# Loading attention's values per pair of heads, more buffers for the squares of the out-projection, and the refill's low parts on one engine

## The chip, the cores and the metric

The kernel runs on one core of a Trainium2 chip. The metric is the device time of one execution in microseconds (us), here the median of three runs. All arithmetic on TensorE (PE) that has to be accurate is done in three passes: a float32 operand is cut into a high part (a rounded copy) and a low part (the difference), and high times high, high times low and low times high are summed. The high part is a cast on ScalarE (ACT), the low part a subtraction on VectorE (DVE) or on GpSimd (POOL). SyncE (SP), ACT and POOL each issue DMA transfers into a queue of their own.

## What is computed

One decoder layer for 2048 tokens of width 1024, with 8 attention heads of 64:

```python
hn = _rmsnorm(h, ln_mix[i])
z = hn @ w_in[i]                                  # q, k, v and the pooling channels u
att = _dilated_attention(q, k, v, slopes)         # windows (128,1), (512,4), (2048,16)
pool = _multiscale_pool(u, pool_w[i], pool_scale[i])
h = h + jnp.concatenate([att, pool], axis=-1) @ w_out[i]
hn = _rmsnorm(h, ln_ffn[i])
up = _causal_dwconv(hn @ w_up[i], conv_w[i], conv_b[i])
gate, val = jnp.split(up, 2, axis=-1)
h = h + (jax.nn.silu(gate) * val) @ w_down[i]
g = jax.nn.sigmoid(_rmsnorm(h, ln_ple[i]) @ w_ple_gate[i])
h = h + g * (p[i] @ w_ple[i])
```

Each head's three dilated branches are summed by weights that come out of their row maxima and denominators.

## The kernel before, in words

The time line of the profiled execution has these stages: projection (0 to 401 us), attention (401 to 737), out-projection (737 to 945), up (945 to 1809), down (1809 to 2300), and gate, per-layer embedding and final norm (to the end).

**Attention** runs 8 heads of NQ = 16 steps each, in four pairs of 32 steps. A step computes the scores of one block (`far_scores`, `near_scores`), their maxima and exponentials, transposes them and multiplies by the values. The near branch reads tiles `v1`, the far ones `v3`, four of each per head. All operands come from DRAM through SP's queue: at the start `load_qk(0) + load_v(0)`, then the list `queue`, to which step 1 of each head appends the eight transfers of `load_qk(h + 1)` (six of 0.5 MB with rows of 8 KB, and the bias tiles `fb` and `nb`) and step 8 the eight of `load_v(h + 1)` (256 KB each, 512 bytes to a row); one is put in SP's queue per step. SP is in order: a transfer whose buffer is not yet free holds all that stand behind it. The score operands have one buffer for even and one for odd heads, so those of head h + 1 are free when head h - 1 ends; `v1` has 7 buffers and `v3` 6.

At the end of a pair, `mix_stats` stores the pair's statistics (`std`, `stf`) and loads them back in another layout (`sn`, `sf`); step 9 of the next pair computes from these (`mix_lift`, DVE tile `lo`), step 10 the weights, stored as `wd` (`mix_weights`). Then, for each of four chunks c, `mix_fetch` loads two tiles `wb` (the weights broadcast over 64 partitions), `mix_products` multiplies them with the sums s1 and s3 into m1 and m3 and adds these, and `mix_store` splits and stores the result. All of the mix's DMAs are issued by POOL, and its products run on POOL too: POOL is in order, so `std` and `stf` of the next pair stand behind the last chunk's products and stores.

**Out-projection.** Four token chunks c, each in two groups of four output tiles. `end(grp)` adds the residual (`xc`), stores h1 and calls `add_square`: ACT squares the tile into `sq`, DVE adds it to `acc`. After each chunk `rms_scale` sums `acc` over the partitions on PE (`st`).

**Up** is 44 turns, in each of which PE multiplies seven products; their operands a11, s2, a12, s1, s3, s4, a22 (normalised states and sums of them) stand in SBUF as high and low parts. The class `Refill` brings operands for the first half (12 of the 24 in a12, s3, a22 are still to come at its first turn) and, at turn NF - 1 to NF + 1, all 56 of the second half: a load by SP, the cast on ACT, the subtraction on POOL for each third (first refill) or each second (second refill), else on DVE. POOL also computes the weight sums of each turn (`sums_t`, `sum_t4`). In the step after the last turn (`over`) the last activations (`yg`) are finished while the first units of down are loaded and split (`unit0`, `unit1`, `unit2`).

Of the kernel before, what the change touches and what calls it, by code (L numbers as in the profile page):

```python
# [49 lines left out]
def fp(ap):  # L50
    return ap.bitcast(F32)
# [433 lines left out]
def phase_attention(tc, g, mx, near_b, far_b):  # L485
# [5 lines left out]
    with ExitStack() as ctx:  # L491
# [27 lines left out]

        def load_v(h):  # L520
            t = heads[h]
            near_v = g.vn.rearrange("n r j h a d -> (r j) n h (a d)")
            far_v = g.vf.rearrange("r (b m) j h a d -> r (m j) b h (a d)", m=4)
            t.v1, t.v3 = [], []
            loads = []
            for q in range(4):
                v1 = sb.tile([P, 4, P], F32R, tag="v1", bufs=7, name=f"v1_{h}_{q}")
                v3 = sb.tile([P, 4, P], F32R, tag="v3", bufs=6, name=f"v3_{h}_{q}")
                loads.append((v1, near_v[:, 4 * q : 4 * q + 4, h, :]))
                loads.append((v3, far_v[q, :, :, h, :]))  # L530
                t.v1.append(v1)
                t.v3.append(v3)
            return loads

# [84 lines left out]
        def near_pv(gi, kbs, first):  # L619
            gr, t, q0 = groups[gi], heads[gi // 4], 4 * (gi % 4)  # L620
            for kb in kbs:
                if q0 + kb < 0:
                    continue
                m0, m1 = max(0, kb), min(3, kb + 1)
                b0, b1 = 4 * m0 + kb + 1, 4 * m1 + kb + 1
                kt = q0 + kb
                for pt in (gr.h, gr.l):
                    nc.tensor.matmul(
                        gr.o[:, m0 * P : (m1 + 1) * P],
                        t.v1[kt // 4][:, kt % 4, :],  # L630
                        pt[:, b0 : b1 + 1 : 4, :],
                        start=first,
                        stop=False,
                        skip_group_check=True,
                    )
                    first = False

        def far_pv(gi, kbs, first):
            gr, t = groups[gi], heads[gi // 4]
            for kb in kbs:  # L640
                for pt in (gr.h, gr.l):
                    nc.tensor.matmul(
                        gr.o[:, kb * P :],
                        t.v3[gi % 4][:, kb, :],
                        pt[:, 6 * kb + 2 : 18 + kb : 5, :],
                        start=first,
                        stop=False,
                        skip_group_check=True,
                    )
                    first = False  # L650
# [67 lines left out]
        with tc.manual_schedule(engines=set(EN.values())):  # L718
            for dst, src in load_qk(0) + load_v(0):
                rdma(nc, dst, src)  # L720
            queue = []
            stages = {
# [3 lines left out]
            for s in range(NS + 10):  # L726
                if s < NS:
                    h, n = divmod(s, NQ)
                    if n == 1 and h + 1 < H:
                        queue += load_qk(h + 1)  # L730
                    if n == 8 and h + 1 < H:
                        queue += load_v(h + 1)
                    if queue:
                        rdma(nc, *queue.pop(0))
                if s == NS + 2:
                    last_far(nc, g, mx, ps_t, pairs[NPAIR - 1])
                    pieces = pairs[NPAIR - 1].pieces = last_weights(nc, mx, pairs[NPAIR - 1])
# [171 lines left out]
def phase_rest(tc, g, mxs, mx, last_pair, xT, pT, w_out, w_up, w_down, w_gate, w_ple, outT):  # L909
# [3 lines left out]
    with ExitStack() as ctx:  # L913
# [255 lines left out]
        for c in range(NCH):  # L1169
# [16 lines left out]
            def begin(grp):  # L1186
# [5 lines left out]
                for j in range(4):  # L1192
                    x = cb.tile([P, CH], F32, tag="xh1", bufs=10, name=f"xc{c}")
                    nc.sync.dma_start(x, xT[4 * grp + j, :, cs])
                    xs.append(x)

            def end(grp):
                for j in range(4):
                    jj = 4 * grp + j
                    nc.vector.tensor_tensor(xs[jj], pss[grp][j], xs[jj], op=ALU.add)  # L1200
                    nc.scalar.dma_start(g.h1[jj][:, cs], xs[jj])
                    add_square(nc, cb, acc, xs[jj], jj == 0)
                    hs.append(xs[jj])
# [113 lines left out]
        class Refill:  # L1317
            def __init__(self, half, names, depth, low):
                self.todo = [(p, k) for p in names for k in range(HK)]
                self.half, self.depth, self.low, self.got, self.n = half, depth, low, [], 0  # L1320

# [10 lines left out]
            def take(self, n=1):  # L1332
                for _ in range(n):
# [10 lines left out]
                    nc.scalar.copy(hi, t)  # L1344
                    (nc.gpsimd if m % self.low == self.low - 1 else nc.vector).tensor_tensor(lo, t, fp(hi), op=ALU.subtract)
                    if m:
# [24 lines left out]
        with tc.manual_schedule(engines=set(EN.values())):  # L1371
            raw_load(1)
            refill = Refill(0, ("a12", "s3", "a22"), 6, 3)
            for _ in range(6):
# [5 lines left out]
            for i in range(len(turns) + 1):  # L1380
# [7 lines left out]
                if i == NF - 1:  # L1388
                    assert not prep
                    refill = Refill(1, ("a11", "s2", "a12", "s1", "s3", "s4", "a22"), 10, 2)  # L1390
                    for _ in range(10):
                        refill.fetch()
# [35 lines left out]
                if prev:  # L1428
                    conv_b(prev.yv, prev.uv, NF + prev.f, prev.half)
                after(1)  # L1430
                if last:
# [55 lines left out]
                after(6)  # L1487
                if over:
                    unit2()
                prev = None if over else cur  # L1490
# [369 lines left out]
```

## Time and profile before

| | us |
|---|---|
| median of three runs | 2545.92 |
| the three runs | 2545.68, 2554.62, 2545.92 |
| profiled execution, its own time | 2557.69 |
| its span | 2555.8 |
| mean granted clock of PE | 0.971 |
| PE busy | 2428.2 (95%) |
| DVE busy | 1589.2 (62%) |
| ACT busy | 1106.9 (43%) |
| POOL busy | 556.7 (22%) |

The profiled execution is 11.8 us longer than the median of the runs and 3.1 us longer than the slowest of them. PE is busy nearly all the time, so what an edit can bring lies in PE's idle stretches and in stretches of a lower granted clock.

### The profile page before, as it was taken

The numbers are of one execution on the slowest core, as the hardware profiler recorded it, in microseconds if no ns is written. First come the engines' busy times: TensorE is split into PE (matmuls) and PEld (weight loads), VectorE is DVE, ScalarE is ACT, GpSimd is POOL, SyncE is SP. The second block draws the span as 40 slices with busy tenths as digits, with TensorE's granted clock in tenths as the row PEclk, the third lists the DMA queues.
The fourth block names the chain that finished last, engine by engine and source line by source line (L and its number), as shares of the span: only waits on it lengthen the run. The fifth ranks groups of instructions, "written<-read, shape, count | busy, mean of one in ns | idle before, by whom it ended". The sixth has DMA issues, their size and how long they took to land.

```text
span 2555.8 us, 31938 instructions
## 1 busy us (share of the span) xinstructions
PE 2428.2 (95%) x11515; PEld 2034.4 (80%) x11515; DVE 1589.2 (62%) x2396; ACT 1106.9 (43%) x1923; POOL 556.7 (22%) x454
## 2 busy tenths in 40 slices
PE   8999999888779998999999999999999999999998
PEld 7888887777667877888887888888788888887788
DVE  6645527867673466888889767666535373444654
ACT  5423327877641134444446444444323243333332
POOL 3312221144420023333343000000122222212010
PEclk9899999999889999999999999999999999999999
DMA  7534358697556664455556433433546464544332
GB/s 241 165 120 177 144 175 257 161 216 161 150 180 206 221 227 155 160 173 186 185 181 198 132 120 120 132 120 111 186 141 217 148 224 151 197 146 143 120 103 87
DMA packets 222831, 424.12 MB, mean 166 GB/s; under 512 B 39904, under 2 KB 82528, under 8 KB 219600
## 3 DMA queue, kind: packets, MB, share of 16 engines
q1 hardware_dynamic: 187616, 368.94, 45.7%
q0 software_dynamic: 18912, 25.75, 3.2%
q10 hardware_dynamic: 16144, 27.38, 2.9%
q8 instruction: 91, 1.49, 0.2%
q14 instruction: 68, 0.56, 0.1%
HBM read 290.01 MB, written 131.89 MB: 165 GB/s over the span
## 4 chain that ended last, share of the span: by engine, by line
PE 74%; DMA 8%; issue 7%; DVE 4%; ACT 2%; POOL 2%; SPq 0%; POOLq 0%; DVEq 0%; ACTq 0%
PE ua L1288 18%; PE uc L1288 9%; PE dn L89 6%; PE dn L90 6%; PE dn L88 6%; PE ub L1288 4%; DMA wb<-wd 4%; PE z L90 4%; PE z L88 4%; PE z L89 4%; PE o L88 2%; PE o L90 2%; PE o L89 2%; PE gp L90 2%; PE gp L88 2%
## 5 line engine op out<-in xcount | busy, mean ns | idle before, releaser
L88 PE MATMUL dn<-ah,hd 128*128 128x512 f32 x704 | 274.8, 390 | 2.7 <-ACT ah L83 2.7
L89 PE MATMUL dn<-al,hd 128*128 128x512 f32 x704 | 274.9, 390 | 1.9 <-DVE al L84 1.9
L90 PE MATMUL dn<-ah,ld 128*128 128x512 f32 x704 | 274.5, 390 | 0.0
L84 POOL TENSOR_TENSOR ld<-rd,hd 128x1024 fp32r<-128x1024 f32 x42 | 101.3, 2413 | 756.2 <-ACT hd L83 745.8
L83 ACT CAST hd<-rd 128x1024 fp32r<-128x1024 f32 x88 | 92.5, 1052 | 264.6 <-PE dn L89 226.2
L84 DVE TENSOR_TENSOR al<-ra,ah 128x512 fp32r<-128x512 f32 x88 | 120.3, 1371 | 134.0 <-ACT ah L83 134.0
L88 PE MATMUL z<-hnh,wh 128*128 128x512 f32 (+1 forms) x480 | 171.2, 357 | 9.7 <-ACT hnh L251 5.8
L89 PE MATMUL z<-hnl,wh 128*128 128x512 f32 (+1 forms) x480 | 170.9, 356 | 2.6 <-DVE hnl L252 2.5
L90 PE MATMUL z<-hnh,wl 128*128 128x512 f32 (+1 forms) x480 | 170.8, 356 | 2.3 <-POOL wl L84 1.7
L88 PEld LDWEIGHTS dn<-ah,hd 128*128 128x128 f32 x704 | 132.6, 188 | 30.8 <-ACT ah L83 3.1
L89 PEld LDWEIGHTS dn<-al,hd 128*128 128x128 f32 x704 | 132.6, 188 | 30.2 <-DVE al L84 2.6
L90 PEld LDWEIGHTS dn<-ah,ld 128*128 128x128 f32 x704 | 132.6, 188 | 27.3
L154 DVE TENSOR_TENSOR acc<-acc,sq 128x512 f32<-128x512 f32 (+1 forms) x125 | 91.9, 735 | 64.9 <-ACT sq L153 52.9
L84 DVE TENSOR_TENSOR wu<-ru,wu 128x1024 fp32r<-128x1024 f32 x88 | 128.2, 1457 | 1.7 <-ACT wu L83 1.7
L1288 PE MATMUL ua<-s2h,wu 128*128 128x512 f32 x352 | 118.3, 397 | 3.4 <-ACT ug L1425 3.4
L1288 PE MATMUL uc<-a22h,wu 128*128 128x512 f32 x352 | 116.8, 393 | 1.8 <-DVE uv L1311 1.8
L1288 PE MATMUL ua<-s4h,wu 128*128 128x512 f32 x352 | 116.7, 393 | 0.2 <-ACT uv L1469 0.2
L1288 PE MATMUL uc<-s3h,wu 128*128 128x512 f32 x352 | 115.8, 390 | 0.0
L1288 PE MATMUL ub<-a12h,wu 128*128 128x512 f32 x352 | 115.6, 389 | 0.0
L1288 PE MATMUL ua<-s1h,wu 128*128 128x512 f32 x352 | 115.5, 389 | 0.0
L1288 PE MATMUL ua<-a11h,wu 128*128 128x512 f32 x352 | 115.5, 389 | 0.0
L88 PEld LDWEIGHTS z<-hnh,wh 128*128 128x128 f32 x480 | 95.3, 199 | 21.8 <-ACT hnh L251 5.8
(334 smaller groups left out, 6498.6 us busy)
## 6 DMA issues: line engine op xcount, KB each, us to landing
rd<-in_w_down_dram SPq DMA_DIRECT2D x88, 512.0 KB, 3.6
ru<-in_w_up_dram SPq DMA_DIRECT2D x66, 512.0 KB, 4.1
act<-yg SPq DMA_DIRECT2D x44, 512.0 KB, 3.1
ra<-act SPq DMA_DIRECT2D x88, 256.0 KB, 3.8
wr<-in_w_in_dram SPq DMA_DIRECT2D x64, 256.0 KB, 4.2
nt<-h SPq DMA_DIRECT2D x56, 256.0 KB, 3.7
h<-h SPq DMA_DIRECT2D x56, 256.0 KB, 5.2
td<-t SPq DMA_DIRECT2D x22, 512.0 KB, 2.6
```

The costliest lines, as they stand in the source:

```text
L83: nc.scalar.copy(hi, src)
L84: (low or nc.gpsimd).tensor_tensor(lo, src, fp(hi), op=ALU.subtract)
L88: nc.tensor.matmul(ps, wh, ah, start=first, stop=False)
L89: nc.tensor.matmul(ps, wh, al, start=False, stop=False)
L90: nc.tensor.matmul(ps, wl, ah, start=False, stop=last)
L154: nc.vector.tensor_tensor(acc[:, :n], acc[:, :n], sq[:, :n], op=ALU.add)
L1288: nc.tensor.matmul(pst, x[:, ksl], y, start=first and k == 0 and n == 0, stop=k == HK - 1 and n == 2, skip_group_check=True)
```

## The change

1. The values of both heads of a pair are loaded at once: tiles of 128 x 4 x 2 x 128, 512 KB each with rows of 1 KB, 32 transfers where there were 64. Buffers: `v3` 4, `v1` 5. A table `V_STEPS` puts each into SP's queue at a step of the pair before: v3 at 24, 28, 32, 36 and v1 at 19, 30, 34, 38. At the start they follow `load_qk(0)` in the order v3, v1.
2. In the out-projection the squares go in turn to the `sq` buffer and to the two `dg` buffers (which also hold the diagonals that `spread_prep` makes once per chunk).
3. All low parts of `Refill` are computed on DVE: 4 subtractions of the first refill and 14 of the second leave POOL.
4. `unit2()` is called in the `over` step ahead of `after(1)` and not at its end.

```diff
-        def load_v(h):
-            t = heads[h]
-            near_v = g.vn.rearrange("n r j h a d -> (r j) n h (a d)")
-            far_v = g.vf.rearrange("r (b m) j h a d -> r (m j) b h (a d)", m=4)
...
-                v1 = sb.tile([P, 4, P], F32R, tag="v1", bufs=7, name=f"v1_{h}_{q}")
-                v3 = sb.tile([P, 4, P], F32R, tag="v3", bufs=6, name=f"v3_{h}_{q}")
...
+        near_v = g.vn.rearrange("n r j (p h) a d -> (r j) n p (h a d)", h=2)
+        far_v = g.vf.rearrange("r (b m) j (p h) a d -> r (m j) b p (h a d)", m=4, h=2)
+        vals = {}
+        def load_v(pr, which, q):
+            v = sb.tile([P, 4, 2, P], F32R, tag=which, bufs=4 + (which == "v1"), name=f"{which}_{pr}_{q}")
+            vals[pr, which, q] = v
+            src = near_v[:, 4 * q : 4 * q + 4, pr, :] if which == "v1" else far_v[q, :, :, pr, :]
+            return v.rearrange("p b h d -> p b (h d)"), src
+        V_STEPS = {n: (("v3", "v1")[x], q) for x in range(2) for q, n in enumerate(((24, 28, 32, 36), (19, 30, 34, 38))[x])}
...
-            for dst, src in load_qk(0) + load_v(0):
+            for dst, src in load_qk(0):
                 rdma(nc, dst, src)
+            for q in range(4):
+                for which in ("v3", "v1"):
+                    rdma(nc, *load_v(0, which, q))
...
-                    if n == 8 and h + 1 < H:
-                        queue += load_v(h + 1)
                     if queue:
                         rdma(nc, *queue.pop(0))
+                    for pr in range(1, NPAIR):
+                        if s - 2 * NQ * (pr - 1) in V_STEPS:
+                            rdma(nc, *load_v(pr, *V_STEPS[s - 2 * NQ * (pr - 1)]))
...
+            squares = itertools.cycle((("sq", 1), ("dg", 2), ("dg", 2)))
+            def square_tile(name):
+                tag, bufs = next(squares)
+                return cb.tile([P, CH], F32R, tag=tag, bufs=bufs, name=name)
...
-                    add_square(nc, cb, acc, xs[jj], jj == 0)
+                    add_square(nc, cb, acc, xs[jj], jj == 0, tile=square_tile)
...
-                    (nc.gpsimd if m % self.low == self.low - 1 else nc.vector).tensor_tensor(lo, t, fp(hi), op=ALU.subtract)
+                    nc.vector.tensor_tensor(lo, t, fp(hi), op=ALU.subtract)
...
+                if over:
+                    unit2()
                 after(1)
...
                 after(6)
-                if over:
-                    unit2()
```

On SP, around the start of pair 1 (the score operands of head 3, qhh, ks, qll, fb, nb, and the values around them), there stood before:

```order
L55 DMA qhh_4693<-qh_82 64x2048
L55 DMA ks_4695<-kh_90 64x2048
L55 DMA qll_4694<-ql_86 64x2048
L55 DMA qhh_4693<-qh_82 64x2048
L55 DMA ks_4695<-kl_94 64x2048
L55 DMA qll_4694<-ql_86 64x2048
L55 DMA fb_4697<-in_far_b_dram 128x512
L55 DMA nb_4696<-in_near_b_dram 128x256
L55 DMA v_3_0_4881<-vn 128x4x128
L55 DMA v_3_0_4882<-vf 128x4x128
L55 DMA v_3_1_4883<-vn 128x4x128
L55 DMA v_3_1_4884<-vf 128x4x128
```

And of the change:

```order
L56 DMA qhh_4671<-qh_82 64x2048
L56 DMA v_1_2_4622<-vf 128x4x256
L56 DMA ks_4673<-kh_90 64x2048
L56 DMA v_1_2_4702<-vn 128x4x256
L56 DMA qll_4672<-ql_86 64x2048
L56 DMA qhh_4671<-qh_82 64x2048
L56 DMA v_1_3_4757<-vf 128x4x256
L56 DMA ks_4673<-kl_94 64x2048
L56 DMA qll_4672<-ql_86 64x2048
L56 DMA v_1_3_4811<-vn 128x4x256
L56 DMA fb_4675<-in_far_b_dram 128x512
L56 DMA nb_4674<-in_near_b_dram 128x256
```

The eight small loads of head 3's values that stood behind its score operands are gone, and four double loads of pair 1 (of which each waits for a buffer of pair 0) stand between the score operands.

On POOL, at the first turns of up (a22l, s3l and a12l are low parts of the first refill, t the weight sums), there stood before:

```order
L1345 TENSOR_TENSOR a12l_9170<-nt,a12h_9169 128x512
L1345 TENSOR_TENSOR s3l_9215<-nt,s3h_9214 128x512
L109 TENSOR_TENSOR pw<-ms,mhalf 128x4
L1345 TENSOR_TENSOR a22l_9257<-nt,a22h_9256 128x512
L1017 TENSOR_TENSOR t_9287<-ru 128x512
L1018 TENSOR_TENSOR t_9287<-ru_9139,ru 128x512
L1019 TENSOR_TENSOR ru<-ru_9139,t_9287 128x512
L1030 TENSOR_TENSOR t_9311<-ru_9139,ru 128x512
L1345 TENSOR_TENSOR a22l_9314<-nt,a22h_9313 128x512
```

On DVE in the same place of the change:

```order
L1355 TENSOR_TENSOR s3l_9189<-nt,s3h_9188 128x512
L1355 TENSOR_TENSOR a22l_9193<-nt,a22h_9192 128x512
L85 TENSOR_TENSOR wu<-t_9068,wu 128x1024
L1355 TENSOR_TENSOR a22l_9216<-nt,a22h_9215 128x512
L1355 TENSOR_TENSOR a22l_9220<-nt,a22h_9219 128x512
L1321 TENSOR_TENSOR uv<-uv,uc 128x512
L85 TENSOR_TENSOR wu<-ru_9053,wu 128x1024
L85 TENSOR_TENSOR wu<-t_9072,wu 128x512
L1355 TENSOR_TENSOR a22l_9250<-nt,a22h_9249 128x512
```

The last a22l, which on POOL stood behind the four weight sums of the turn, now stands on DVE behind two splits of weights.

On DVE in the `over` step (ld and al are low parts of down's third unit, yg the last activations), of the change:

```order
L1318 SCALAR_TENSOR_TENSOR yv<-halo,vec,yv 128x2
L85 TENSOR_TENSOR ld_2_15399<-rd,hd_2_15398 128x1024
L85 TENSOR_TENSOR al<-ra,ah 128x512
L1311 SCALAR_TENSOR_TENSOR yg<-ug,vec,yg 128x1023
L85 TENSOR_TENSOR ld_3_15458<-rd_3_15455,hd_3_15457 128x1024
L1312 SCALAR_TENSOR_TENSOR yg<-ug,vec,yg 128x1022
L1317 SCALAR_TENSOR_TENSOR yg<-halo,vec,yg 128x1
L1318 SCALAR_TENSOR_TENSOR yg<-halo,vec,yg 128x2
L1495 TENSOR_TENSOR yg<-yg,yv 128x1024
```

Before, the two ld and the al stood behind the last row; now three splits stand ahead of the end of yg.

## Rows read from the trace of the kernel before

**Rows 1.** The page's chain that ended last, by line, shares of the span.

```profile
PE ua L1288 18%; PE uc L1288 9%; PE dn L89 6%; PE dn L90 6%; PE dn L88 6%; PE ub L1288 4%; DMA wb<-wd 4%; PE z L90 4%; PE z L88 4%; PE z L89 4%; PE o L88 2%; PE o L90 2%; PE o L89 2%; PE gp L90 2%; PE gp L88 2%
```

**Rows 2.** Windows of attention: length, busy us (instructions) by engine, clock, DMA share, GB/s.

```profile
490.00:530.00 40.00, 35.52 (x225) 31.40 (x226) 33.19 (x107) 34.96 (x97) 14.10 (x15) 1.00 0.74 157
530.00:570.00 40.00, 33.02 (x206) 28.64 (x206) 29.01 (x86) 30.91 (x87) 19.73 (x20) 1.00 0.90 216
570.00:610.00 40.00, 29.47 (x171) 26.48 (x172) 24.07 (x79) 26.03 (x73) 18.66 (x22) 0.79 0.59 129
...
650.00:690.00 40.00, 25.21 (x135) 22.73 (x135) 20.35 (x68) 20.93 (x58) 17.65 (x20) 0.70 0.48 128
```

**Rows 3.** PE's timeline: start, us, instruction, in brackets idle time before and releaser.

```profile
580.44 0.58 PE L572 MATMUL sn<-ks,qhh 128*128 128x256 f32 x1 [8.30 <-DVE st L577]
...
670.21 0.58 PE L572 MATMUL sn<-ks,qhh 128*128 128x256 f32 x1 [6.17 <-DVE st L577]
```

**Rows 4.** Longest pieces of the chain through 400:745 us: start, us, what.

```profile
507.18 26.49 DMA wb<-wd
...
540.62 25.26 DMA wb<-wd
...
571.89 4.24 DMA std<-sx
...
629.13 28.23 DMA wb<-wd
```

**Rows 5.** Waits in 400:745 us: total us, times, longest.

```profile
DVE lo L841 <- DMA sf<-stf: 17.9, 2, 9.8
```

**Rows 6.** Tile wb, all eight loads in 675:720 us.

```profile
DMA to landing us min/median/max: 8.0/9.4/10.8
```

**Rows 7.** SP's timeline in 495:560 us: issue of the transfers.

```profile
506.83 0.45 SPq L55 DMA_DIRECT2D qhh<-qh  x1
...
526.32 7.45 SPq L55 DMA_DIRECT2D v<-vf  x1
...
542.91 0.45 SPq L55 DMA_DIRECT2D qhh<-qh  x1
```

**Rows 8.** Tile fb in 414:420 us, head 1's bias: issue and landing.

```profile
L55 SPq DMA_DIRECT2D fb<-in_far_b_dram x1: 585/585/585, 414.5 to 414.5; - x1
...
DMA to landing us min/median/max: 15.7/15.7/15.7
```

**Rows 9.** PE's timeline where head 1's scores begin.

```profile
434.26 0.33 PE L572 MATMUL sn<-ks,qhh 128*128 128x256 f32 x1
```

**Rows 10.** Timeline of all engines, end of the out-projection's first chunk.

```profile
808.24 0.69 DVE L154 TENSOR_TENSOR acc<-acc,sq 128x512 f32<-128x512 f32 x1 [0.70 <-ACT sq L153]
...
811.76 1.65 PE L99 MATMUL st<-ones,acc 128*128 128x1 f32 x8 [1.94 <-DVE acc L154]
```

**Rows 11.** PE's timeline, end of the second chunk, and up's first turn.

```profile
908.18 1.87 PE L99 MATMUL st<-ones,acc 128*128 128x1 f32 x8 [2.94 <-DVE acc L154]
...
950.87 0.50 PE L1288 MATMUL ua<-s2h,wu 128*128 128x512 f32 x1 [3.17 <-ACT ug L1425]
...
978.45 0.79 PE L1288 MATMUL uc<-a22l,wu 128*128 128x512 f32 x1 [4.96 <-POOL a22l L1345]
```

**Rows 12.** POOL's timeline at up's first turn.

```profile
976.15 2.24 POOL L1345 TENSOR_TENSOR a22l<-nt,a22h 128x512 fp32r<-128x512 f32 x1
```

**Rows 13.** PE's timeline in 1394:1412 us, the second refill.

```profile
1402.70 0.79 PE L1288 MATMUL ua<-s4l,wu 128*128 128x512 f32 x1 [4.59 <-DVE s4l L1345]
...
1404.14 0.63 PE L1288 MATMUL ua<-s4l,wu 128*128 128x512 f32 x1
...
1407.74 0.39 PE L1288 MATMUL ua<-a11l,wu 128*128 128x512 f32 x1
```

**Rows 14.** DVE's timeline in the second refill.

```profile
1365.77 1.79 DVE L1345 TENSOR_TENSOR a11l<-nt,a11h 128x512 fp32r<-128x512 f32 x1
```

**Rows 15.** PE's timeline at the start of down.

```profile
1820.29 0.50 PE L89 MATMUL dn<-al,hd 128*128 128x512 f32 x1 [0.97 <-DVE al L84]
```

More of the change, by code (lines that the diff above doesn't have):

```diff
@@ L1 @@
+import itertools
 import math
@@ L518, in load_qk @@
             return loads
-        def load_v(h):
-            t = heads[h]
-            near_v = g.vn.rearrange("n r j h a d -> (r j) n h (a d)")
-            far_v = g.vf.rearrange("r (b m) j h a d -> r (m j) b h (a d)", m=4)
-            t.v1, t.v3 = [], []
-            loads = []
-            for q in range(4):
-                v1 = sb.tile([P, 4, P], F32R, tag="v1", bufs=7, name=f"v1_{h}_{q}")
-                v3 = sb.tile([P, 4, P], F32R, tag="v3", bufs=6, name=f"v3_{h}_{q}")
[L529 to L533, printed above, removed]
+        near_v = g.vn.rearrange("n r j (p h) a d -> (r j) n p (h a d)", h=2)
[7 more added lines that the diff above has]
+        V_STEPS = {n: (("v3", "v1")[x], q) for x in range(2) for q, n in enumerate(((24, 28, 32, 36), (19, 30, 34, 38))[x])}
         def begin(s):
@@ L619, in near_pv @@
         def near_pv(gi, kbs, first):
-            gr, t, q0 = groups[gi], heads[gi // 4], 4 * (gi % 4)
+            gr, q0 = groups[gi], 4 * (gi % 4)
             for kb in kbs:
@@ L629, in near_pv @@
                         gr.o[:, m0 * P : (m1 + 1) * P],
-                        t.v1[kt // 4][:, kt % 4, :],
+                        vals[gi // 8, "v1", kt // 4][:, kt % 4, gi // 4 % 2, :],
                         pt[:, b0 : b1 + 1 : 4, :],
@@ L638, in far_pv @@
         def far_pv(gi, kbs, first):
-            gr, t = groups[gi], heads[gi // 4]
+            gr = groups[gi]
             for kb in kbs:
@@ L643, in far_pv @@
                         gr.o[:, kb * P :],
-                        t.v3[gi % 4][:, kb, :],
+                        vals[gi // 8, "v3", gi % 4][:, kb, gi // 4 % 2, :],
                         pt[:, 6 * kb + 2 : 18 + kb : 5, :],
@@ L1317, in phase_rest, with __init__ @@
         class Refill:
-            def __init__(self, half, names, depth, low):
+            def __init__(self, half, names, depth):
                 self.todo = [(p, k) for p in names for k in range(HK)]
-                self.half, self.depth, self.low, self.got, self.n = half, depth, low, [], 0
+                self.half, self.depth, self.got, self.n = half, depth, [], 0
             def fetch(self):
@@ L1372, in phase_rest @@
             raw_load(1)
-            refill = Refill(0, ("a12", "s3", "a22"), 6, 3)
+            refill = Refill(0, ("a12", "s3", "a22"), 6)
             for _ in range(6):
@@ L1389, in phase_rest @@
                     assert not prep
-                    refill = Refill(1, ("a11", "s2", "a12", "s1", "s3", "s4", "a22"), 10, 2)
+                    refill = Refill(1, ("a11", "s2", "a12", "s1", "s3", "s4", "a22"), 10)
                     for _ in range(10):
```

## The prediction

> **What bounds the kernel now.** I read the page's chain of work first: nearly all of it is PE, in the order of the products, and the only transfer with a share of its own is the load of wb in attention, 4% of the span [rows 1]. So the question for each part of the change is where PE stands still, and which wait ends last there. I then went through attention window by window. In an undisturbed stretch (490 to 530 us) PE does 225 matmuls in 40 us at full clock; in 530 to 570 it does 206, in 570 to 610 171 and in 650 to 690 135, the latter two at clocks of 0.79 and 0.70, that is partly at the lower of its two levels [rows 2]. The missing 19 + 54 + 90 = 163 matmuls at 40/225 us each are 29 us lost in attention. PE's timeline shows the two holes: the longest waits in them, 8.30 and 6.17 us, end with DVE's maxima st [rows 3], and DVE in turn stood in mix_lift, which waited 17.9 us in two times for the reloaded statistics sf [rows 5]. Both holes lie at the start of a pair.
>
> The chain through attention says why sf is late. wb loads of 26.49 (issued 507.18) and 25.26 us (issued 540.62) follow each other, the second lands at 565.88, and only after the products that it releases does POOL come to std, at 571.89 [rows 4]. PE goes on at 580.44 [rows 3], 14.6 us after that landing. A pair later the same happens (629.13 + 28.23). In 675 to 720, where head 7 is the last and no further score operands are fetched, all eight wb land in 8.0 to 10.8 us [rows 6]. The slow ones were issued together with a burst of score operands on SP's queue: these bursts start at 506.83 and 542.91 [rows 7], a head apart, which makes (542.91 - 506.83)/16 = 2.26 us a step.
>
> **The change part by part.** *Values.* The bytes stay the same; what moves is where they stand. Behind the burst of 506.83 the values of the next head followed, and the queue filled: the load of 526.32 took 7.45 us to issue, until 533.77 [rows 7], and the wb of 507.18 landed at 533.67, the same moment [rows 4]. The burst is six transfers of 0.5 MB and 0.4 MB of bias, 3.5 MB; with the 1.2 MB of values behind it 4.7 MB went in 27 us, 174 GB/s, between the windows' 157 and 216 [rows 2]. In the change one load of 0.5 MB stands beside that burst and the next comes 8 steps (18 us) after its start: 4.0 MB at 174 GB/s are through at 530. I take the landing of the first late wb as 3 to 8 us earlier, so that the wb of the last chunk goes out at 533 to 537 rather than 540.62, and ahead of the next burst. Undisturbed it would take 9.4 us [rows 6] and land at 542 to 547. mix_lift is due 9 steps after 542.91, at 563, and the way from that landing to PE's restart is 14.6 us: 557 to 562, no stall. If it still meets the burst it takes 25 us again, lands at 558 to 562, and PE restarts at 573 to 577 rather than 580.44, which takes back 3 to 8 of each hole. The next burst is broken up by the double loads, of which three wait for buffers of the running pair, so the long rows come in two portions; that speaks for the quicker case. Bounds: all 29 us gone, or none. I take 21 gone and 8 left, since the transfers of both cases are the same in bytes and some meeting stays likely.
>
> The start pays for it: before head 1's score operands now stand 4.2 MB of values instead of 2.1. fb was issued at 414.5 and landed at 430.2 [rows 8]; its first use was 434.26 [rows 9]. 2.1 MB more at 216 GB/s, the most in [rows 2], would be 10 us; less, as head 1's own values of before partly ran beside it: I take 7. fb comes at 437: a stall of about 3 us (0 to 6).
>
> *Squares.* With one buffer, square and sum alternate: DVE waits 0.70 us for each next square, and PE waits 1.94 for the last sum [rows 10]. With three buffers the sums follow at DVE's 0.69 us; three of the 0.70 go, more than the 1.94: all of it. At the second chunk's end PE waits 2.94 [rows 11], but DVE also normalises there; I take 1.5. At the third, whose sums stand ahead of up's first low parts, 3.17 [rows 11], of which I take 2, since loads for the refill come at the same time. Sum 5.4, bounds 0 and 8.05 (all three waits). The diagonals in the dg buffers move behind the next chunk's squares; PE asks for them much later, so this is hidden; its price, if the cover is gone, is one 0.7 us write.
>
> *Refill, first.* PE waits 4.96 us for a22l [rows 11], computed on POOL from 976.15 in 2.24 us behind the four weight sums [rows 12]. DVE does it in 0.69 [rows 10] (a sum of the same shape) and has it two places behind a cast; that ends near 973.5, when PE asks. The wait and some 2 us of lower clock behind it go, less a remainder: 5 (3 to 7). *Second.* PE waits 4.59 us for s4l, and the matmuls behind take 0.63 instead of 0.39 us for a while [rows 13], another 1.9 us. POOL's 14 subtractions, here moved, cost DVE 14 x 0.69 = 9.7 us, eleven of them, 7.6, ahead of s4l. But a DVE subtraction beside a POOL one took 1.79 us [rows 14] where it takes 0.69 alone, and about ten DVE instructions ahead of s4l are longer by such a 1.1 us at most: 10. Net 2.4 us earlier or a little more, since DVE's instructions overlap at their ends: with the lower clock behind the wait I take 4 of the 6.5 (0 to 6.5).
>
> *unit2.* The 0.97 us for al [rows 15] goes; but three splits now stand ahead of the last yg, whose store stands on SP ahead of the next units' loads, and these come later by about as much. I take 0 (-2 to +1).
>
> Sum against the profiled execution: 2557.69 - 21 + 3 - 5.4 - 5 - 4 = 2525.3. That execution is 11.8 us above the median, and nothing in the page tells which stage varies: if it is the late wb, which the change takes away, 2525 stands, if anything else, it is 2513. I take half: **2519 us**.
>
> **Rivals.** *A, the forecast*, some of the stalls left: 2506 to 2531. *B, the stalls go wholly*: 8 us less, 2511. *C, the stalls stay.* The wb of 507.18 was in flight with the burst's 8 KB rows, and the change leaves the burst where it was; then only the small parts count: 2557.69 - 14.4 + 3 = 2546, with half the offset 2540 (2531 to 2547). For it: the bytes on SP's queue until 533 are nearly the same. Against: the wb landed at the end of the values, not of the burst. A rule speaks for C: the Trainium skill, "DMA: Bandwidth & Descriptors", section "Queues, rings and completion order", says that a DMA engine takes turns between its queues a packet at a time. By that, long packets of SP's burst hold each packet of wb back and short ones of the values hardly do, and removing the values removes little. No run so far separates the two; the 8 to 10.8 us landings without a burst fit it. *D, slower*: the double loads that wait for buffers hold the score operands behind them, so that the burst at a pair's start stretches from 20 to 30 us, the last wb lands with its end, at 573, and each hole grows by 7; with 6 at the start and only half of the small parts: 2557.69 + 14 + 6 - 7 = 2571, with half the offset 2565. It needs the last wb to land after 570 to decide. *E, DVE becomes the bound in the second refill*: the 9.7 us are not given back; the gain of 4 is lost and s4l is later by 4: 8 us more than A, 2527.
>
> **How the numbers follow.** About 12.7 us (0.5%) is what these runs can tell from no change, so faster means below 2533. Chances: A 0.37, B 0.22, C 0.27, D 0.08, E 0.06. A, B and E are faster, a quarter of C too, which makes 0.72; 0.03 of A and E reach beyond 2533 and go to no change, so faster 0.69, no change 0.23 with C's rest, slower 0.08. The likeliest is A. The range goes down to 2557.69 less all 29 and the upper bounds of the small parts (8 + 7 + 6.5) less the offset, 2495, and up past C's middle, 2543; D lies outside.
>
> **What would show it.** Right: the waits of mix_lift for sf near zero, the windows of attention at 220 matmuls each and full clock, wb landings below 15 us for the last chunk, std issued before 560; no wait at the first chunk's st; a22l and s4l without waits of over 1 us. A wait of some 3 us at the first matmul of head 1 would confirm the price at the start. Wrong, if wb's landings near the bursts stay at 20 to 28 us (C), or if qhh or ks of the second half of a burst are waited for (D), or if DVE's backlog in the second refill moves the wait from s4l to s3l or a22l (E).

## The result and the profile after

The change takes 2527.34 us in the median of seven runs (2521.96 to 2537.44), the kernel before 2545.92 (2539.4 to 2554.62, seven runs beside them): a ratio of 0.9926, with a 95% interval of 0.9902 to 0.9951, or 18.6 us. The profiled execution of the change took 2537.44 us (span 2535.3), so it too lies some 10 us above the median of its kernel, as that of before did.

Stage by stage, from the first matmul of each stage in PE's timeline of the two profiled executions (us):

| stage | before | after | difference |
|---|---|---|---|
| attention | 337.95 | 336.87 | -1.1 |
| out-projection | 205.49 | 199.66 | -5.8 |
| up | 864.59 | 853.02 | -11.6 |
| down | 490.15 | 490.62 | +0.5 |
| gate to end | 256.25 | 254.41 | -1.8 |

So the gain lies in the out-projection and in up, and nearly nothing of it in attention, where I had put 18 of 32 us. PE's timeline of the change (start, us, instruction, idle time and releaser) shows that the two holes of [rows 3] are still there and as long in sum. A hole had two parts before; the first parts, which stand ahead of the waits in [rows 3], were:

```profile
568.23 0.39 PE L628 MATMUL o<-pth,v 128*128 128x256 f32 x1 [3.56 <-DVE s L658]
...
659.72 0.58 PE L628 MATMUL o<-pth,v 128*128 128x256 f32 x1 [7.39 <-DVE s L658]
```

That makes 11.9 and 13.6 us. In the change each hole is one wait:

```profile
435.76 0.55 PE L573 MATMUL sn<-ks,qll 128*128 128x256 f32 x1 [1.82 <-DMA qll<-ql]
...
581.45 0.58 PE L572 MATMUL sn<-ks,qhh 128*128 128x256 f32 x1 [11.60 <-DVE st L577]
667.72 0.58 PE L572 MATMUL sn<-ks,qhh 128*128 128x256 f32 x1 [11.39 <-DVE st L577]
```

The windows that answer to [rows 2] have the first hole wholly in the third one:

```profile
530.00:570.00 40.00, 35.59 (x224) 30.87 (x222) 30.75 (x93) 32.68 (x92) 22.73 (x24) 1.00 0.90 202
570.00:610.00 40.00, 26.05 (x158) 23.25 (x158) 24.12 (x79) 25.46 (x72) 15.67 (x17) 0.83 0.63 150
...
650.00:690.00 40.00, 26.16 (x153) 23.08 (x152) 22.37 (x73) 23.65 (x67) 13.78 (x16) 0.83 0.55 144
```

The chain through 400 to 745 us, beside [rows 4], says what happened:

```profile
508.70 24.59 DMA wb<-wd
...
540.22 18.90 DMA wb<-wd
...
565.21 11.69 DMA std<-sx
...
627.79 14.79 DMA wb<-wd
...
648.68 12.92 DMA std<-sx
```

The wb of the last chunk is faster (18.90 and 14.79 us where 25.26 and 28.23 stood), and std goes out at 565.21 rather than 571.89, and at 648.68. But it now takes 11.69 and 12.92 us to land, where it took 4.24 at the first of the two places. DVE waits even longer for sf than before (in [rows 5] it was 17.9 us), by the list of waits:

```profile
DVE lo L845 <- DMA sf<-stf: 24.0, 2, 12.1
```

What std met is in SP's timeline of the change:

```profile
544.66 0.45 SPq L56 DMA_DIRECT2D qhh<-qh  x1
...
556.28 0.37 SPq L56 DMA_DIRECT2D v<-vf  x1
556.69 0.55 SPq L56 DMA_DIRECT2D ks<-kl  x1
...
559.15 0.36 SPq L56 DMA_DIRECT2D v<-vn  x1
561.44 1.83 SPq L56 DMA_DIRECT2D fb<-in_far_b_dram  x1
```

The last transfer of that burst went out, in the kernel before, at:

```profile
548.49 0.50 SPq L55 DMA_DIRECT2D nb<-in_near_b_dram  x1
```

The burst that began at 542.91 [rows 7] and was all issued within some 6 us now begins at 544.66, waits at the load of 556.28 for a buffer of the running pair, and sends a second portion from there on, with two double loads of values. std is issued into the middle of that portion.

In the other stages the waits that I had priced are gone or small. PE's timeline of the change, for [rows 11], [rows 13] and [rows 15]:

```profile
901.96 1.05 PE L100 MATMUL st<-ones,acc 128*128 128x1 f32 x8 [1.01 <-DVE acc L155]
...
957.90 0.50 PE L1298 MATMUL uc<-s3l,wu 128*128 128x512 f32 x1 [0.94 <-DVE s3l L1355]
966.53 0.50 PE L1298 MATMUL uc<-a22l,wu 128*128 128x512 f32 x1 [0.17 <-DVE a22l L1355]
...
1384.61 0.50 PE L1298 MATMUL ua<-s4l,wu 128*128 128x512 f32 x1 [1.69 <-DVE s4l L1355]
...
1809.19 0.80 PE L89 MATMUL dn<-ah,hd 128*128 128x512 f32 x1 [4.48 <-ACT ah L84]
```

The wait of 1.94 us at the first chunk's st [rows 10] has no successor in it. The waits for a22l (4.96), s4l (4.59) and the second st (2.94) are 0.17, 1.69 and 1.01.

### The profile page after: what moved, and what is told of

Read it like the earlier page. It is cut to its first block, busy times and chain, and to the rows that moved or that the text cites. A ratio compares the mean times of both kernels' runs of the same rounds, so it can differ in the third digit from the quotient of the medians.

```text
span 2535.3 us, 31890 instructions
## 1 busy us (share of the span) xinstructions
PE 2417.9 (95%) x11515; PEld 2026.2 (80%) x11515; DVE 1579.9 (62%) x2414; ACT 1106.6 (44%) x1923; POOL 527.8 (21%) x436
## 4 chain that ended last, share of the span: by engine, by line
PE 74%; DMA 8%; issue 7%; DVE 4%; ACT 2%; POOL 2%; SPq 0%; POOLq 0%; DVEq 0%; ACTq 0%
PE ua L1298 18%; PE uc L1298 9%; PE dn L89 6%; PE dn L90 6%; PE dn L91 6%; PE ub L1298 4%; PE z L91 4%; PE z L89 4%; PE z L90 4%; DMA wb<-wd 3%; PE o L91 2%; PE o L89 2%; PE o L90 2%; PE gp L89 2%; PE gp L90 2%
## 5 line engine op out<-in xcount | busy, mean ns | idle before, releaser
L85 DVE TENSOR_TENSOR ld<-rd,hd 128x1024 fp32r<-128x1024 f32 x46 | 56.7, 1233 | 90.4 <-ACT hd L84 90.4
```

The lines of the kernel that those rows point to most:

```text
L85: (low or nc.gpsimd).tensor_tensor(lo, src, fp(hi), op=ALU.subtract)
```

## The experiments

**Which part carries the gain.** The first two kernels split the change. e1 is the change with `tile=square_tile`, the refill's rule and the place of `unit2()` as before; e2 is the kernel before with these three as in the change:

```diff
-                    add_square(nc, cb, acc, xs[jj], jj == 0)
+                    add_square(nc, cb, acc, xs[jj], jj == 0, tile=square_tile)
...
-                    (nc.gpsimd if m % self.low == self.low - 1 else nc.vector).tensor_tensor(lo, t, fp(hi), op=ALU.subtract)
+                    nc.vector.tensor_tensor(lo, t, fp(hi), op=ALU.subtract)
...
+                if over:
+                    unit2()
                 after(1)
```

> Only the paired value loads are kept; squares, refill and unit2 are as before. Theory (the loads bring the last wb in earlier, but the store of the statistics, std, then meets the second portion of the split burst of score operands, so that the holes at the pair starts stay at 11 to 12 us each): attention within 3 us of before, total 0 to 4 us below before, ratio 0.998 to 1.000. Rival (the loads are worth the 18 us that I forecast, and the profiled execution of the change is only an unlucky one): ratio 0.993, holes of 4 us or less.

Measured: 2545.2 us against 2547.43, ratio 0.9988 (0.9973 to 1.0003). The paired loads alone bring nothing that can be told from zero, and 18 us are excluded. On the stage and the holes the theory missed in part: attention is 332.3 us in this execution, 5.7 less than in that of before, and of the two holes one is long and one short, in PE's timeline:

```profile
582.10 0.58 PE L572 MATMUL sn<-ks,qhh 128*128 128x256 f32 x1 [13.07 <-DVE st L577]
662.23 0.58 PE L572 MATMUL sn<-ks,qhh 128*128 128x256 f32 x1 [4.65 <-DVE st L577]
```

> The other three parts alone, values loaded per head as before. Theory (they carry the whole gain): out-projection 5 to 6 us shorter, up 11 to 12 us shorter, total 16 to 19 us below before, ratio 0.993, the same as the change. Rival (values carry the larger part): ratio 0.996 or above.

Measured: 2525.86 us, ratio 0.9918 (0.9897 to 0.9938): the whole gain, or a little more. Up is 853.7 us long, as in the change, the out-projection 194.8; attention, whose program is that of before, is 331.5 us, with the late wb of before around the first hole, by the chain:

```profile
503.63 25.93 DMA wb<-wd
536.51 28.08 DMA wb<-wd
570.62 2.82 DMA std<-sx
```

Here wb is late and std short, in the change wb is shorter and std long, and the first hole comes out alike (5.50 + 6.55 us here, 11.60 there). At the second hole, 7.79 us, even this execution has a wb of 15.30 and a std of 9.72 us, as the change has. By the medians of e1 and e2 the three other parts carry the gain.

One profiled execution says less about attention than it seems to. The program of attention is the same before, in e2 and in e11, and the stage took 338.0, 331.5 and 335.6 us, its second hole 13.6, 7.8 and 14.6; it is the same in the change and in e1, with 336.9 and 332.3 us, and 11.4 and 4.65. A hole in one execution can differ by some 7 us for no edit at all, so the worth of an edit is taken from the medians below, and the holes only show where it acts.

**The squares by themselves.** Kernel e11 is the kernel before with the first two lines of the diff above.

> The kernel before with the squares' buffers alone. Theory: the waits of 1.94 and 2.94 us at the first two chunks' ends and of 3.17 at up's first product go to below 1.2 each, and nothing else moves: out-projection 5 to 6 us shorter, up's start 3 to 5, total 8 to 11 less than before, ratio 0.9960. Rival (what the squares no longer wait for, the loads behind them do): out-projection 5 to 6 us shorter, but up longer by as much as the wait at its start was, total 4 to 6 less, ratio 0.998.

Measured: 2538.32 us against 2546.85, ratio 0.9967 (0.9949 to 0.9984), 8.4 us; the interval, 4 to 13 us, has room for both totals. The out-projection is 196.8 us long, 8.7 less than before; up is 864.3, the same as before: the rival was right on up and the size of the first stage was larger than either said. Of the waits for st the first is gone, the second is 2.00 us, not below 1.2. PE's timeline shows why up gains nothing: the 3.17 us before s2h are gone, and the operands behind are waited for instead, s3l, which had 0.61 us before, and still a22l:

```profile
952.73 0.80 PE L1295 MATMUL uc<-s3l,wu 128*128 128x512 f32 x1 [2.02 <-DVE s3l L1352]
964.65 0.50 PE L1295 MATMUL uc<-a22l,wu 128*128 128x512 f32 x1 [1.96 <-POOL a22l L1352]
```

Up is 863.6 us with the paired loads alone (e1), 864.3 with the squares alone and 853.7 with squares, refill and unit2 (e2). So its 11 us come with the refill's low parts on top of the squares. That is by exclusion: no run has the refill without the squares, or unit2 by itself.

**Is std late because of its place on POOL?** e3 is the change with chunk 3 of pairs 0 and 1 multiplied and stored four steps later, which puts `std` and `sn` ahead of them on POOL; e4 is e2 with the same lines:

```diff
                         mix_fetch(nc, g, mx, nc.gpsimd, pr, pairs[pr], c)
+                    if c == NCH - 1 and pr < NPAIR - 2:
+                        d -= 4
                     if d == CFG["m"][2] + CFG["m"][3] * c + CFG["m"][4]:
```

> The change, and the products and the store of chunk 3 of pairs 0 and 1 four steps later, so that POOL issues std and stf ahead of them. Theory (std is late because it stands behind the last wb on POOL, and then meets the burst): std goes out at the pair's start, 16 to 20 us earlier, lands within 12 us even beside the burst, mix_lift does not wait, the two holes of 11.6 and 11.4 us fall to 3 us or less each; 15 to 22 us less than the change. Rival (the burst holds every small POOL transfer for as long as it lasts, wherever it is issued): sf arrives as late as now, holes of 8 us or more stay, at most 6 us less than the change.

Measured: 2518.46 us, ratio 0.9886 (0.9866 to 0.9905); 9 us less than the change, between the two theories, and the two intervals just touch. PE's holes shrink to less than half:

```profile
570.73 0.58 PE L572 MATMUL sn<-ks,qhh 128*128 128x256 f32 x1 [4.09 <-DVE st L577]
651.82 0.58 PE L572 MATMUL sn<-ks,qhh 128*128 128x256 f32 x1 [5.22 <-DVE st L577]
```

POOL's timeline has std going out at the pair's start and its landing, and tile sf the time of the way back:

```profile
545.61 0.55 POOL L765 DMA_DIRECT2D std<-sx  x1
...
558.18 0.83 POOL L769 DMA_DIRECT2D sn<-std  x1 [11.52 <-DMA std<-sx]
559.01 0.77 POOL L773 DMA_DIRECT2D sf<-stf  x1
```

```profile
DMA to landing us min/median/max: 8.7/10.7/11.5
```

The place on POOL was half of it. The other half is the round trip itself, out and back: sf, issued at 559.01, lands 10.7 us later, 24 us after std went out, and 23 us at the next pair. The lift is due after nine steps, 20 us; the difference is about the hole that is left.

> As e2 (values per head, the other three parts as in the change) with chunk 3 of pairs 0 and 1 four steps later. Theory: std goes out at the pair's start here too; it meets an unsplit burst and the values of the next head behind it and lands within 20 us, so the holes fall to 5 us or less each: 12 to 22 us less than e2. If the values per pair then have a worth of their own, it shows as the difference to e3: theory 0 to 5 us in favour of e3, from shorter landings beside the queue. Rival as in e3: no more than 6 us less than e2.

Measured: 2523.06 us, ratio 0.9903 (0.9881 to 0.9925), 2.8 us less than e2 with intervals that overlap, where I had expected 12 to 22. std did go out at 545.58, and POOL then stood for 21 us until it had landed; chunk 3 was behind it, and DVE's next sums, which write the buffer that chunk 3 still had to read, stood behind that. From POOL's and DVE's timelines:

```profile
567.62 0.83 POOL L766 DMA_DIRECT2D sn<-std  x1 [20.98 <-DMA std<-sx]
```

```profile
572.00 0.68 DVE L659 TENSOR_TENSOR s<-o,ev 64x512 f32<-64x512 f32 x1 [10.62 <-POOL m L884]
```

The wait only changed its name. At the same place std takes 21.6 us here, beside the values per head and a burst issued at once, and 12.1 in e3, beside the paired values and the split burst. That is no clear worth of the paired loads: the reload is then quicker here (3.4 us for sf), and the round trip is 26 us in e4 and 24 in e3.

**More time for the lift.** e5 shifts the mix of pairs 0 and 1 by three steps, on the change; e6 does it on e2:

```diff
-                d = s - (pr + 1) * 2 * NQ
+                d = s - (pr + 1) * 2 * NQ - (3 if pr < NPAIR - 2 else 0)
```

> The change, and the whole mix of pairs 0 and 1 three steps later (lift at step 12 of the next pair, not 9), which also puts chunk 3 behind std on POOL. In e3 std and then sn and sf took 10 to 12 us each beside the burst, 21 in sum against the 20 that nine steps give. Theory: twelve steps give 27, so mix_lift finds sf there; the holes of 4.1 and 5.2 us in e3 fall to 2 or less, 6 to 10 us less than e3, near 2510. Rival: POOL, waiting for std, holds chunk 3's products back beyond the time when the next pair's first sums need the buffers of s1 and s3 (the wait of DVE for POOL seen once in e4, 10.6 us): a hole of 3 us or more by that wait, and no gain on e3.

Measured: 2562.23 us, ratio 1.0069 (1.0051 to 1.0087), slower than before. The rival was right, at eight times its price. Every chunk moved, so that three wb and not one were issued with the burst (at 507.6, 508.4 and 509.2, landing after 16.0, 29.2 and 32.7 us); std went out at 568.97, POOL stood for it, and chunk 3 came at 588.5. From PE's timeline:

```profile
592.03 0.58 PE L628 MATMUL o<-pth,v 128*128 128x256 f32 x1 [25.26 <-DVE s L658]
```

> As e5 with the values loaded per head. In e4 std took 21 us beside the unsplit burst and the values behind it, and DVE's sums waited 10 us for chunk 3. Theory (how long std takes at a pair's start is what the values per pair change): std again 18 to 22 us, holes of about 10 us by DVE's wait for POOL stay, within 4 us of e4, and 8 us or more above e5. Rival (the two loadings are worth the same once std goes out on time): within 4 us of e5.

Measured: 2550.51 us, ratio 1.0022 (1.0011 to 1.0033). The same hole, 20.2 and 19.1 us long; neither expectation holds:

```profile
583.77 0.58 PE L629 MATMUL o<-pth,v 128*128 128x256 f32 x1 [20.21 <-DVE s L659]
```

Here std took 5.4 and 5.9 us, where e5 has 17.5 and 20.6, and it was chunk 2 that came late, so the worth of the paired loads can't be read from this pair of runs.

e9 tries it more narrowly: e3, and only the lift and the weights of pairs 1 and 2 two steps later.

```diff
-                if d == CFG["m"][0]:
+                if d == CFG["m"][0] + 2 * (pr > 0):
...
-                if d == CFG["m"][1]:
+                if d == CFG["m"][1] + 2 * (pr > 0):
```

> e3, with mix_lift and mix_weights of pairs 1 and 2 two steps later (11 and 12 in place of 9 and 10), everything else in e3's order; unlike in e5, chunks 0 to 2 stay ahead of std. In e3 the round trip of the statistics beside the burst took 21 us against 20 of nine steps, and holes of 4.1 and 5.2 us were left. Theory: 24.9 us are enough, the holes fall below 1.5, some 8 us less than e3, near 2510, the fastest so far. Rival (what waits at the pair's start is no longer the lift but the chain of chunk 3 on POOL, whose buffers the sums need): the wait only changes its name, and the time stays within 3 us of e3.

Measured: 2531.73 us (2516.01 to 2539.39), ratio 0.9946 (0.9925 to 0.9967). The hole at the start of pair 2 is gone, as the theory had it, and the one at pair 3 is 25 us long, the rival's wait, on DVE for the buffer of the sums:

```profile
664.19 0.58 PE L628 MATMUL o<-pth,v 128*128 128x256 f32 x1 [25.05 <-DVE s L658]
```

Weights that come two steps later send their wb into the next burst a chunk earlier: the three from 580.66 on overlap it, two of them take 29.5 and 31.0 us, and all chunks behind are late. Both theories were half right: the lift's wait ends with two more steps, but the steps are missing at the next burst, and the price is 13 us over e3 where the rival had at most 3.

**Burst or values?** e7 and e8 leave out the loads of one kind: in e7 heads 2 to 7 use the score operands of heads 0 and 1, in e8 pairs 1 to 3 use the values of pair 0.

```diff
+            if h >= 2:
+                heads[h] = heads[h - 2]
+                return []
```

```diff
-                            rdma(nc, *load_v(pr, *V_STEPS[s - 2 * NQ * (pr - 1)]))
+                            which, q = V_STEPS[s - 2 * NQ * (pr - 1)]
+                            vals[pr, which, q] = vals[0, which, q]
```

> The change without the loads of the score operands and biases of heads 2 to 7: these heads use those of heads 0 and 1, so the output is not the layer's. Theory (the bursts slow wb, std and sn): all wb land within 13 us, std and sf within 5, no hole of over 2 us at a pair's start, attention 20 to 25 us shorter than in the change. Rival (the values' short rows slow them as much): wb at 18 us or more in part, holes of 5 us or more.

Measured (one execution): 2506.7 us, no hole, attention 309.8 us, 27 less than the change and 28 less than before, close to the 29 us that the prediction counted as lost there. All 24 wb, with the values still on the queue:

```profile
DMA to landing us min/median/max: 6.9/9.0/11.9
```

> The change without the values' loads of pairs 1 to 3: these use pair 0's, so the output is not the layer's. Theory (bursts): a wb issued with a burst still takes 17 us or more, as long as 3.5 MB need, and std, if issued inside a burst, 8 us or more; holes smaller than in the change since bursts end sooner, but not zero. Rival (it is the values on the queue that make wb late): all wb within 13 us, no holes.

Measured (one execution): 2510.23 us, attention 313.9. The first wb issued with a burst takes as long as ever, the last chunk's no longer, and no hole of over 2 us is left; DVE waits 2.3 us once for sf. From the chain:

```profile
506.29 24.53 DMA wb<-wd
537.75 11.22 DMA wb<-wd
555.03 9.68 DMA std<-sx
```

The burst makes a wb late by itself (24.53 without any values, 24.59 with them). In the next pair the wb issued with the burst, at 582.5, took 17.2 us (25.8 in the change): it went out 1.2 us ahead of the burst's first transfer and not 0.2. The values matter at the pair's start, where they break the burst up and lengthen it: the burst of 542.2 is all issued by 547.2 here, that of 544.66 in the change by 563.99.

**Long packets or many bytes?** e10 is the change with each large load of a score operand in two halves:

```diff
-                loads.append((t.qhh[hs], g.qh[pr][rows]))
-                loads.append((t.ks[hs], (g.kh if half == 0 else g.kl)[pr][rows]))
-                loads.append((t.qll[hs], g.ql[pr][rows]))
+                for x in range(2):
+                    cs, ns = slice(x * 1024, x * 1024 + 1024), slice(2 * x, 2 * x + 2)
+                    loads.append((t.qhh[hs, cs], g.qh[pr][rows, cs]))
+                    loads.append((t.ks[hs, ns], (g.kh if half == 0 else g.kl)[pr][rows, ns]))
+                    loads.append((t.qll[hs, cs], g.ql[pr][rows, cs]))
```

> The change with each of the six large loads of score operands cut into two halves with rows of 4 KB in place of 8 KB, two put in the queue per step: the same bytes, fourteen transfers in place of eight. If the length of the packets decides (a turn of POOL's queue waits for one packet of SP's): the wb issued with a burst falls from 24 to 26 us to 19 or less, std beside the burst from 12 to 8 or less, holes of 11 us to 6 or less, 8 us or more less than the change. If only the bytes ahead decide: landings within 3 us of the change, and its time too.

Measured: 2517.4 us, ratio 0.9892 (0.9858 to 0.9925), 10 us less than the change by the medians, with intervals that overlap. The chain and PE's timeline:

```profile
507.74 17.88 DMA wb<-wd
...
554.30 10.08 DMA std<-sx
```

```profile
574.33 0.58 PE L574 MATMUL sn<-ks,qhh 128*128 128x256 f32 x1 [6.52 <-DVE st L579]
```

With the same bytes the wb beside the first burst lands in 17.88 us. Undisturbed it is 9.4 [rows 6], so the 15.2 us that the burst cost it in the change have fallen to 8.5, about half, with rows of half the length. std gained less (10.08 against 11.69). But the edit changed a second thing: the issue of that burst is spread over three times as long. First and last transfer on SP, in the change and then in e10:

```profile
508.81 0.45 SPq L56 DMA_DIRECT2D qhh<-qh  x1
...
514.06 0.43 SPq L56 DMA_DIRECT2D nb<-in_near_b_dram  x1
```

```profile
506.78 0.45 SPq L56 DMA_DIRECT2D qhh<-qh  x1
...
524.23 0.33 SPq L56 DMA_DIRECT2D nb<-in_near_b_dram  x1
```

And other wb tell against the length of the rows as the only cause. With rows of 8 KB one of e1, issued 1.0 us ahead of its burst, landed in 15.71 us; with rows of 4 KB one of e12 (below), issued 3.4 us into its burst, took 24.08, by the two chains:

```profile
595.51 15.71 DMA wb<-wd
```

```profile
584.53 24.08 DMA wb<-wd
```

So e10 shows what the edit did to the landings, and not which of the two did it, the shorter rows or the slower issue.

**Both edits that gained.** e12 is e10 with the lines of e3.

> The change with both edits that gained: the burst in halves with rows of 4 KB (e10) and chunk 3 of pairs 0 and 1 behind std on POOL (e3). Theory: with short landings the statistics' round trip of about 18 us (e10: std 10, sf 8.5) now begins at the pair's start and ends before the lift is due after 20; the holes of 6.5 and 6.4 us in e10 go to below 2, 8 to 12 us less than e10 and e3: 2508, ratio 0.985 to 0.987. Rival (std at the pair's start meets the burst's first portion and takes longer than later, and chunk 3 behind it makes DVE wait for the buffers of the sums): a hole of 4 us or more at one of the pairs, 2515 or more.

Measured: 2514.31 us against 2545.53, ratio 0.9887 (0.9868 to 0.9906). One hole is gone, of the other 3.63 us are left:

```profile
645.77 0.39 PE L574 MATMUL sn<-ks,qhh 128*128 128x256 f32 x1 [3.63 <-DVE st L579]
```

By the median it is the lowest kernel of the study, 13 us below the change; by its interval it can't be told from e3 and e10. The holes fell as the theory said, to 0 and 3.6 us; the time, by the medians, fell by 3 to 4 us instead of 8 to 12.

## Why the prediction was right in the total and wrong in a term

The forecast was 2519 us (2495 to 2543) and faster; it is 2527 and faster. The total is right, its division among the parts is not, and that they come out so near is in good part luck. The values and the start, -18 us together, brought nothing. In their place the three other parts brought 21.6 us by the medians of e2 where I had 14.4, and the whole offset of the profiled execution, 11.8 us, has to be taken off, of which I took half.

*Values, -21 in attention.* This term failed. Its first steps held in part: the first wb that meets the burst landed 1.9 us sooner (24.59 for 26.49; I had 3 to 8), and the last chunk's went out at 540.22, not at 533 to 537. It landed at 559.1, as in my case "still meets the burst" (558 to 562). The step that broke is the next: "the way from that landing to PE's restart is 14.6 us". I carried this over from the trace of before as if it were a fixed latency. It contains a store and a load on the same POOL queue, which before came after the burst had drained; issued 6.7 us earlier they meet the second portion of the split burst, and the way is 581.45 - 559.1 = 22.3 us. I had counted the splitting of the burst as a help and had not asked what else stands in the stretch into which its rest is moved; rival D had the stretched burst, but on the score operands and the last wb, not on std. e3 and e8 show both halves: with std ahead of chunk 3 the holes fall to 4 and 5 us, without the values to below 2. The worth of the paired loads in the kernel as it stands is 0.9988 (e1), not 18 us. For attention that is rival C, at about a quarter of the chance; its time, 2531 to 2547, was not met either, since the small parts gave more.

*The signs.* Of those that were to show the forecast right, the ones of attention failed: DVE's waits for sf are 24.0 us and not near zero, the windows with the holes have 158 and 153 matmuls and not 220, the last chunk's wb takes 18.90 us in one pair, and only in the other, with 14.79, the less than 15 that I asked for, and std goes out at 565.21 and not before 560. The ones of the small parts held (no wait at the first st, 0.17 us for a22l), but for s4l with 1.69 us instead of at most 1.

*Why the burst slows wb.* The prediction left open whether the values, the bytes or the long rows do it. It is the burst: without the bursts no wb is late (e7, 11.9 us at most), and without the values the first one is as late as with them (e8, 24.53). So what I held against rival C, that the wb of before landed as the values came to their end, was a coincidence. Bytes or rows stays open, since e10 changes the rows and the spread of the issue together. The Trainium skill, "DMA: Bandwidth & Descriptors", section "Queues, rings and completion order", has the rule that a DMA engine changes queues a packet at a time. The 17.88 us of e10 fit it, and so does the first wb of e8, but no run here shows it by itself.

*The start, +3.* PE waits 1.82 us for head 1's qll in the change and 2.55 in e1: right in size; the wait is for qll, two transfers ahead of the fb that I had named.

*Squares, -5.4.* 1.94 and 2.94 us became 0 and 1.01, and the out-projection is 5.8 (change), 8.7 (e11) and 10.7 us (e2) shorter. The rest over the waits is in part the lower clock behind them: the granted clock of the stage is 0.94 before, 0.96 in the change and 0.97 in e11 and e2, and 6.8 us at the lower level behind each of the two waits are none and 3.4 in the change. The three runs differ among themselves by 5 us; the change has a wait of 2.48 us for hwo at 753.08 that e2 has not. The 2 us for the third wait are not there by themselves (e11): they passed to s3l.

*Refill, -5 and -4.* Up is 11.6 us shorter, against 11 with the 2 us of the squares' tail: right in sum. Of the second wait 1.69 us are left, where the 2.4 us of net gain would leave 2.2.

*unit2, 0.* PE waited 0.97 + 2.70 + 0.90 us for al, ah and al in this place before, and waits 4.48 for ah now: right in size, though no run has unit2 by itself.

*The offset of the profiled execution.* I took half of its 11.8 us away for stalls that would go. The stalls did not go, and the change's own runs spread by 15 us. Against the medians the three parts gave 21.6 us (e2) where I had 14.4. In the stages of the profiled executions they come to 5.8 + 11.6 - 0.5, or 16.9 us, nearer to it.

## What to carry to other kernels

A latency read from a trace holds for the traffic beside it: when an edit moves a small store or load to another time, look up what is on the DMA engines then, before its duration is used again. A wait that ends with a load on an in-order queue has more than one thing behind it; list all that stands behind it, buffers to be freed included, since curing the first one (e4, e5, e9) makes the next one the bound. And where small transfers share the DMA engines with a burst, a burst in smaller pieces (e10, shorter rows and a slower issue together) and the small ones' place in their queue (e3) were each worth about 10 us by the medians, which the two gains together did not add up to (e12), while loading the same bytes in fewer, larger transfers was worth nothing that these runs can tell from zero. Last, a term that fails can hide in a total that comes out right: compare stage by stage before believing the sum.

## What the runs showed of the hardware

A DVE copy of two columns became short when POOL's subtractions left. From DVE's and POOL's timelines of the kernel before, and from DVE's of the change:

```profile
1376.81 1.26 DVE L1305 COPY halo<-ug 128x2 f32<-128x2 f32 x1
```

```profile
1376.63 1.41 POOL L1345 TENSOR_TENSOR a12l<-ndg,a12h 128x512 fp32r<-128x512 f32 x1 [0.83 <-ACT a12h L1344]
```

```profile
1362.12 0.16 DVE L1315 COPY halo<-ug 128x2 f32<-128x2 f32 x1
```

The copy began 0.18 us after POOL's subtraction and ended 0.03 us after it; it is 1.1 us longer than that of the change. Of the 44 copies of the kernel before four are that long, and four each in e1 and e11, which kept POOL's subtractions; each of the twelve began while POOL subtracted and ended within 0.04 us of it. In the other runs, without these subtractions on POOL, none is. So the length of the POOL instruction that is under way, not its own, sets such a wait. And a small POOL store (std, 64 x 128) took between 2.4 us (before, at 663.4) and 21.6 us (e4, at 545.58), according to what SP had in flight.
